# The rotated partner of mixer C's queries and keys, from four transfers within SBUF

## The chip, the cores and the metric

The kernel runs on one core of one Trainium2 chip. The metric is the device time of one execution in microseconds; the lower one is the better one. The kernel before takes 1890.34 us (median of three runs, 1889.98 to 1893.89).

## What is computed

The reference is a trunk of two layers over 512 tokens of 2,048 features, all in float32. Each layer norms its input with a modulation that is computed from a vector `c`, projects it once to 6,656 columns, runs four kinds of attention on disjoint columns, gates their outputs and projects them back. Cut to the parts that the change meets:

```python
for i in range(DEPTH):                                   # 2
    mod = silu(c) @ w_ada[i] + b_ada[i]
    h = rms_norm(x, norm_w[i]) * (1 + scale) + shift
    proj = h @ w_in[i]                                   # 2048 x 6656
    y_a, y_b, y_c, y_d = four mixers on their columns    # 8 heads of 64 each
    y = concat(y_m * silu(z_m) for the four mixers)
    x = x + gate * (y @ w_out[i])
return rms_norm(x, final_norm_w)

def apply_rope(x, cos, sin):         # mixer C: q (8 heads) and k (2 heads), after rms_norm
    x0, x1 = x[..., 0::2], x[..., 1::2]                  # adjacent pairs of a head
    return stack([x0 * cos - x1 * sin, x0 * sin + x1 * cos], -1)
```

The angles depend on the token's row (first 16 pairs of a head) or column (last 16 pairs) in a grid 64 wide. Scores are sums over a head's 64 features, so any order of the features that is the same in q and k gives the same scores.

## The kernel before

Activations lie with features on the 128 partitions and the 512 tokens along the row. The weights come as blocks of 128 x 128, eight to a load (`wst`, 512 KB). A block times an activation tile is a *step*; it takes three matmuls, since weights and activations are each split into a high and a low part (`wh`, `wl`, `hh`, `hl`): ACT copies the high part, DVE subtracts to get the low part (`w_conv`, line 185). There are 2,224 steps: 52 output tiles of the input projection and 16 of the output projection, 16 steps each, twice, and some halved ones. The trace names their PSUM tiles `pj0qD`, `pj1o` and so on: layer, kind, mixer.

The program is written by a planner that runs at build time. `slot` (line 147) emits four steps, 12 matmuls, and among them the pieces of other work, which are generators that say after how many slots, and at which of the places 0 to 4 in the slot, they go on. A *unit* (line 958) is the attention of one head for 128 queries: scores `s` on PE, then on DVE the bias and the row's extreme (for mixer C a maximum), the exponential on ACT, a reciprocal on DVE, the scaling on ACT; two slots after the scores come the transposes `pt` on PE, then a copy on ACT and a subtraction on DVE, and with every second unit the value products `o`. At most one unit starts in a slot, and only while `lag` is under `THR[0]`, 2000. `lag` is the planner's own account: `Meter` (line 89) adds an assumed price for each instruction that goes through it, and at a slot's end (line 168) `lag` grows by DVE's sum and falls by PE's, or by 1000 if that is more.

A finished projection is worked off by a generator of its kind: `ev_rope` for q and k of mixer C (line 869), `ev_q`, `ev_k`, `ev_v`, `ev_z`. One starts in a slot, and until it is through, its PSUM bank of eight is held. They need SBUF buffers from rings: `tmp` (4), `qs` (6), and `b4` (11 of 4 KB a partition), which holds keys, values, transposed probabilities and the tiles of `w_ada`. `ev_k` waits until 2 + `RES` = 6 of `b4` are free (line 790), `ev_v` for mixers B and D until 5 are (line 797); a unit with an even number takes two of them at its transposes. `ada_tick` (line 263) streams `w_ada` through `b4` and gives DVE its products. Before a projection tile is opened, `open_proj` (line 714) puts in empty slots, with no steps, until three PSUM banks are free.

After the first weight group a scheduler may still move instructions against each other; each engine then works its own list in order. All loads are issued by SP. Every compute instruction has line 101 in the trace, since `Meter` records it there (line 105 in the changed program).

In `ev_rope` the square goes to `sq` and the normed weight times the input to `qw`; `st` sums squares per head on PE, and `ro` is the product of `qw` with a 128 x 128 sign matrix `rot`, which puts minus x1 in the place of x0 and x0 in that of x1. DVE then forms `ro` times sine, `qw` times cosine and their sum; the rotation is done for 5 tiles in each layer, 10 in all.

Of the kernel before, what the change touches and what calls it, by code (L numbers as in the profile page):

```python
# [18 lines left out]
F32 = mybir.dt.float32  # L19
# [3 lines left out]
ALU = mybir.AluOpType  # L23
# [39 lines left out]
NP, TP, LP, VP = (0, 1), (1, 0), (0, 1), (1, 2)  # L63
THR = (2000, 1200)
MAGIC = float(0x5F3759DF)


def col0(name):
# [43 lines left out]
class Trunk:  # L112
# [249 lines left out]
    def setup(self):  # L362
        nc, io, p = self.nc, self.io, self.p
        names = (("c", 16), ("nw", 32), ("bada", 96), ("qw", 2), ("kw", 2), ("fw", 16), ("sink", 16))
        vt = p.tile([128, sum(n for _, n in names)], F32, name="vec")
        nc.sync.dma_start(vt, io["vec"])
        self.vec, o = {}, 0
        for n, k in names:
            self.vec[n] = vt[:, o:o + k]
            o += k  # L370
        ct = p.tile([128, 128 + 128 + 112 + 2 + 1], F32, name="cst")
        nc.sync.dma_start(ct, io["cst"])
        self.ident, self.rot, self.maskb, self.bones = ct[:, :128], ct[:, 128:256], ct[:, 256:368], ct[:, 368:370]
        self.ones = ct[:, 370:371]
        self.x = []
        for k in range(KT):
            t = p.tile([128, 512], F32, name=f"x{k}", tag="y", bufs=16)
            nc.sync.dma_start(t, io["xT"][k * 128:(k + 1) * 128, :])
            self.x.append(t)
        self.ada_seq = []  # L380
        for k in range(KT):
            self.ada_seq += [(0, 16 + k, 0), (0, 16 + k, 1), (0, k, 0), (0, k, 1)]
        self.ada_seq += [(0, 32 + k, hf) for k in range(KT) for hf in range(2)]
        self.ada_seq += [(1, k, hf) for k in range(48) for hf in range(2)]
        self.ada_issued = self.ada_done = 0
        self.ada_t = deque()
        self.ada_every = None
        self.ada_last = 0
        self.ada_keep = 0
        self.ada_dma(4)  # L390
        self.wst, self.wc, self.wdma, self.wcn = {}, {}, 0, 0
        for g in range(2):
            self.w_dma(g)
        self.half1 = p.tile([128, 48], F32, name="half1")
        self.mod = [p.tile([128, 48], F32, name=f"mod{l}") for l in range(NL)]
        self.am = [p.tile([128, 16], F32, name=f"am{l}") for l in range(NL)]
        self.nsink = p.tile([128, 16], F32, name="nsink")
        self.ccol = p.tile([128, 16], F32, name="ccol")
        self.cond = p.tile([128, D], F32, name="cond")
        self.cos = p.tile([128, 512], F32, name="cos")  # L400
        self.sin = p.tile([128, 512], F32, name="sin")
        nc.scalar.activation(self.ccol, self.vec["c"], AF.Tanh, scale=0.5)
        nc.vector.scalar_tensor_tensor(self.ccol, self.ccol, 1.0, self.vec["c"], op0=ALU.add, op1=ALU.mult)
        nc.vector.tensor_scalar(self.nsink, self.vec["sink"], -1.0, None, op0=ALU.mult)
        rows = [self.new_ps(f"cr{q}") for q in range(4)]
        for q in range(KT):
            nc.tensor.matmul(rows[q // 4][:, (q % 4) * 128:(q % 4 + 1) * 128], self.ccol[:, q:q + 1].to_broadcast([128, 128]),
                             self.ident, start=True, stop=True)
        for k in range(KT):
            self.add_square(self.x[k], k)  # L410
            if k % 4 == 3:
                q = k // 4
                nc.scalar.activation(self.cond[:, q * 512:(q + 1) * 512], rows[q], AF.Copy)
        self.end_ps(4)
        ps = self.new_ps("warm")
        self.keep_warm(ps, self.x[KT - WARM[0]:KT])
        self.end_ps()
        self.ada_do()
        self.ada_do()
        self.rstd = self.rms_rows((self.ada_do, self.ada_do, lambda: self.ada_am(0)))  # L420
        self.ada_dma(DEPTH0)
# [447 lines left out]
    def ev_rope(self, l, kind, j, ps, rel):  # L869
# [5 lines left out]
        nc.scalar.activation(sq, ps, AF.Square)  # L875
        nc.scalar.activation(qw, ps, AF.Copy, scale=w)
        rel()
        yield 1, 1
        while self.ps_free < 2:
            yield 1, 1  # L880
        st = self.new_ps(f"st{self.uid()}")
        for i in range(4):
            nc.tensor.matmul(st[:, 2 * i:2 * i + 2], sq[:, i * 128:(i + 1) * 128], self.bones, start=True, stop=True)
        r = self.p.tile([128, 16], F32, name=f"rq{self.uid()}", tag="rq", bufs=6)
        pr = self.new_ps(f"ro{self.uid()}")
        nc.tensor.matmul(pr, self.rot, qw, start=True, stop=True)
        self.r_tmp.put()
        yield 0, 3
        self.rsqrt(st[:, :8], 8, 1.0 / 64, 0.125 if kind == "q" else 1.0, r[:, :8], nc.gpsimd)
        nc.vector.tensor_tensor(tr, pr, self.sin, op=ALU.mult)  # L890
        self.end_ps(2)
        yield 1, 3
        nc.vector.tensor_tensor(qw, qw, self.cos, op=ALU.mult)
        nc.vector.tensor_tensor(tr, tr, qw, op=ALU.add)
        self.r_tmp.put()
# [233 lines left out]
def constants():  # L1129
    onehot, d = bucket_onehot()  # L1130
    n = np.abs(d)
    gmask = np.zeros((16, 1024), np.float32)
    gmask[:8] = np.where(n <= 128, 0.0, NEG)
    cnt = (n <= 64).astype(int) + ((n <= 256) & (n % 4 == 0)) + (n % 16 == 0)
    gmask[8:] = np.where(cnt > 0, np.log(np.maximum(cnt, 1)), NEG)
    dw = np.arange(16)[:, None]
    mb = np.full((16, 112), NEG, np.float32)
    for o, blk, w0, n_ in ((0, 0, 0, 32), (32, 1, 0, 48), (80, 3, 32, 32)):
        w = 16 * blk + dw
        key = (w0 if blk != 1 else 0) + np.arange(n_)[None, :]  # L1140
        st = np.clip(w - 8, 0, 48)
        mb[:, o:o + n_] = np.where((key >= st) & (key < st + 16), 0.0, NEG)
    rot = np.zeros((128, 128), np.float32)
    for i in range(0, 128, 2):
        rot[i + 1, i] = -1.0
        rot[i, i + 1] = 1.0
    bones = np.zeros((128, 2), np.float32)
    bones[:64, 0] = 1.0
    bones[64:, 1] = 1.0
    cst = np.concatenate([np.eye(128, dtype=np.float32), rot, np.tile(mb, (8, 1)), bones,  # L1150
                          np.ones((128, 1), np.float32)], 1)
    t = np.arange(L)
    inv = (np.float32(10000.0) ** (-np.arange(0, 32, 2, dtype=np.float32) / np.float32(32))).astype(np.float32)
    ang = np.concatenate([(t // 64).astype(np.float32)[:, None] * inv, (t % 64).astype(np.float32)[:, None] * inv], 1)
    idx = (np.arange(128) % 64) // 2
    return {"onehot": onehot, "gmask": gmask, "cst": np.ascontiguousarray(cst.astype(np.float32)),
            "cos": np.ascontiguousarray(np.cos(ang).astype(np.float32).T[idx]),
            "sin": np.ascontiguousarray(np.sin(ang).astype(np.float32).T[idx])}


def lay_out(inp, steps):
    g = {k: np.asarray(v) for k, v in inp.items()}
    w = np.empty((NSTEP, 128, 128), np.float32)
    for s, (mat, l, t, k) in enumerate(steps):
        c = col0(t) if mat == "in" else 128 * t
        w[s] = g["w_in" if mat == "in" else "w_out"][l, k * 128:(k + 1) * 128, c:c + 128]
    pad = np.zeros((NL, 8, 15, 63), np.float32)
    pad[..., 16:47] = g["na_rpb"]
    rpb = np.stack([pad[..., 15 - dw:63 - dw] for dw in range(16)], 2)
    cols = lambda a: a.reshape(a.shape[0], -1, 128).transpose(2, 0, 1).reshape(128, -1)  # L1170
    vec = np.concatenate([
        cols(g["c"]), cols(g["norm_w"]), cols(g["b_ada"]), np.tile(g["q_norm_w"], (1, 2)).T, np.tile(g["k_norm_w"], (1, 2)).T,
        cols(g["final_norm_w"][None]), np.broadcast_to(g["attn_sink"].reshape(1, 16), (128, 16))], 1)
    wada = np.ascontiguousarray(g["w_ada"].reshape(NL, 2, 1024, 48, 128).transpose(0, 3, 1, 4, 2))
    arrays = {
        "w": np.ascontiguousarray(w.reshape(NGRP, GW, 128, 128).transpose(0, 2, 1, 3)).reshape(NGRP, 128, GW * 128),
        "wada": wada,
        "xT": np.ascontiguousarray(g["x"][0].T),
        "c": np.ascontiguousarray(g["c"]),
        "vec": np.ascontiguousarray(vec),  # L1180
        "rpb": np.ascontiguousarray(rpb.reshape(NL, 128, 15, 48)),
        "t5": np.ascontiguousarray(g["t5_table"]),
    }
    arrays.update(constants())
    return arrays


SHAPES = {"w": (NGRP, 128, GW * 128), "wada": (NL, 48, 2, 128, 1024), "xT": (D, L), "c": (1, D), "vec": (128, 180),
          "rpb": (NL, 128, 15, 48), "t5": (32, 16), "onehot": (32, 1024), "gmask": (16, 1024), "cst": (128, 371),
          "cos": (128, 512), "sin": (128, 512)}  # L1190


# [17 lines left out]
```

## Time and profile before

| | us |
|---|---|
| median of three runs | 1890.34 |
| profiled execution | 1894.71 |
| its span, first to last instruction | 1892.9 |
| PE busy in the span | 1854.4 (98%) |
| DVE busy | 1356.3 (72%) |
| ACT busy | 1078.2 (57%) |
| chain that ended last: PE's share | 88% |
| 20 matmuls of `ro`, median of one | 0.634 |

The profile is one execution. A matmul is pipelined and its end is modelled, so what one costs in the stream is read from the starts around it, not from its duration. A product in plain float32 stands in the trace as two instructions, one in the program. The program's list orders instructions and tells no times; the trace tells the times.

### The profile page before, as it was taken

What the parts mean: (1) busy time and instruction counts of PE and PEld (TensorE: products, weight loads), DVE (VectorE), ACT (ScalarE), POOL (GpSimd) and SP (SyncE); (2) the same over time, 40 slices, a digit from 0 to 9 for tenths busy, and PEclk for the clock granted to TensorE, in tenths of its full rate; (3) what the DMA queues carried; (4) which work ended last, traced back from release to release, by engine and by line L of the source; (5) the groups of instructions that cost most, each with busy time, mean ns of one, the idle gap of its engine ahead of it and who ended that gap; (6) DMA issues with size and microseconds to landing.
All of it is one profiled execution on the core that took longest, in us unless ns stands there. A gap on an engine that the chain in (4) does not pass through costs nothing.

```text
span 1892.9 us, 26325 instructions
## 1 busy us (share of the span) xinstructions
PE 1854.4 (98%) x9256; PEld 1546.5 (82%) x9256; DVE 1356.3 (72%) x2861; ACT 1078.2 (57%) x2186; POOL 59.5 (3%) x144
## 2 busy tenths in 40 slices
PE   7999999999999999999999999999999999999997
PEld 5787788888888888888778888888888888888887
DVE  7998988787676768977776775577757666655336
ACT  5342457777777776622245773477656666655333
POOL 0001110100000000000000000210000000000000
PEclk8999999999999999999999999999999999999999
DMA  9897544251133226688833333322334342232335
GB/s 335 320 347 233 203 164 135 91 189 60 65 97 109 94 87 223 241 280 305 285 105 129 122 124 139 111 79 90 112 120 127 111 128 89 88 99 89 134 120 181
DMA packets 91459, 291.44 MB, mean 154 GB/s; under 512 B 10208, under 2 KB 17888, under 8 KB 91328
## 3 DMA queue, kind: packets, MB, share of 16 engines
q1 hardware_dynamic: 91328, 289.76, 45.2%
q8 instruction: 73, 1.20, 0.3%
q14 instruction: 58, 0.48, 0.1%
HBM read 278.57 MB, written 11.16 MB: 153 GB/s over the span
## 4 chain that ended last, share of the span: by engine, by line
PE 88%; DVE 7%; DMA 2%; ACT 2%; issue 2%; SPq 0%; DVEq 0%; ACTq 0%
PE pj1o L101 9%; PE pj0o L101 8%; PE o L101 5%; PE s L101 5%; PE pt L101 4%; DVE b L101 3%; PE pj0qB L101 2%; PE pj1zA L101 2%; PE pj1zC L101 2%; PE pj0kB L101 2%; PE pj1zB L101 2%; PE pj1qB L101 2%; PE pj1vD L101 2%; PE pj1qC L101 2%; PE pj1zD L101 2%; PE pj1qA L101 2%
## 5 line engine op out<-in xcount | busy, mean ns | idle before, releaser
L101 ACT ACTIVATE wh<-wst 128x512 fp32r<-128x512 f32 x556 | 346.5, 626 | 398.4 <-PE pj1o L101 77.3
L101 DVE TENSOR_TENSOR wl<-wst,wh 128x512 fp32r<-128x512 f32 x556 | 383.7, 691 | 261.9 <-ACT wh L101 227.1
L101 ACT ACTIVATE P<-P,sm 128x512 f32<-128x512 f32 (+2 forms) x384 | 245.7, 641 | 135.2 <-DVE sm L101 133.5
L101 PE MATMUL s<-b,qs 128*128 128x512 f32 (+2 forms) x512 | 158.9, 392 | 0.2 <-DVE sm L101 0.2
L101 DVE TENSOR_TENSOR b<-pt,b 128x512 fp32r<-128x512 f32 (+2 forms) x256 | 149.4, 584 | 0.8 <-ACT b L101 0.3
L101 DVE CUSTOM_DVE_ANT_0 b<-b,cond,vec 128x1024 f32<-128x1024 f32 x96 | 123.3, 1285 | 28.5 <-DMA b<-wada 28.2
L101 PEld LDWEIGHTS o<-b,b 128*128 128x128 f32 x896 | 124.5, 190 | 13.3 <-DVE b L101 2.9
L101 PEld LDWEIGHTS pt<-cst,P 128*128 128x128 f32 x832 | 106.7, 140 | 34.6 <-ACT P L101 1.3
L101 PE MATMUL pt<-cst,P 128*128 128x128 f32 x832 | 132.4, 272 | 0.9 <-ACT P L101 0.9
L101 ACT ACTIVATE b<-pt 128x512 fp32r<-128x512 f32 (+2 forms) x256 | 129.8, 507 | 2.3
L101 DVE CUSTOM_DVE_ANT_0 b<-b,cond,half 128x1024 f32<-128x1024 f32 x96 | 122.9, 1280 | 4.6 <-DMA b<-wada 3.7
L101 PE MATMUL o<-b,b 128*128 128x256 f32 (+1 forms) x896 | 123.7, 278 | 2.3 <-DVE b L101 2.3
L101 PE MATMUL pj1o<-yh,wh 128*128 128x512 f32 (+1 forms) x304 | 108.6, 357 | 0.0
L101 PE MATMUL pj1o<-yl,wh 128*128 128x512 f32 (+1 forms) x304 | 108.2, 356 | 0.0
L101 PE MATMUL pj1o<-yh,wl 128*128 128x512 f32 (+1 forms) x304 | 108.2, 356 | 0.0
L101 PE MATMUL pj0o<-yh,wl 128*128 128x512 f32 x256 | 100.4, 392 | 1.1 <-DVE wl L101 1.1
L101 PE MATMUL pj0o<-yh,wh 128*128 128x512 f32 x256 | 100.0, 391 | 0.0
L101 PE MATMUL pj0o<-yl,wh 128*128 128x512 f32 x256 | 99.8, 390 | 0.0
L101 DVE TENSOR_TENSOR ot<-o,ot 64x256 f32<-64x256 f32 x109 | 46.0, 422 | 56.0 <-ACT ot L101 54.7
L101 DVE RECIPROCAL sm<-sm 128x1 f32<-128x1 f32 x256 | 41.5, 162 | 62.0 <-ACT P L101 59.2
L101 PEld LDWEIGHTS s<-b,qs 128*128 128x128 f32 x512 | 78.9, 190 | 2.2 <-DVE sm L101 0.4
L101 ACT ACTIVATE P<-s,sm,rq 128x512 f32<-128x512 f32 x64 | 49.8, 778 | 44.2 <-DVE sm L101 43.9
(365 smaller groups left out, 4409.7 us busy)
## 6 DMA issues: line engine op xcount, KB each, us to landing
wst<-w SPq DMA_DIRECT2D x278, 512.0 KB, 3.5
b<-wada SPq DMA_DIRECT2D x192, 512.0 KB, 6.1
T<-btab SPq DMA_DIRECT2D x16, 448.0 KB, 5.3
T<-gtab SPq DMA_DIRECT2D x16, 448.0 KB, 5.0
x<-xT SPq DMA_DIRECT2D x16, 256.0 KB, 5.4
tmp<-xT SPq DMA_DIRECT2D x16, 256.0 KB, 5.5
xs<-xn SPq DMA_DIRECT2D x16, 256.0 KB, 2.5
out<-xn SPq DMA_DIRECT2D x32, 128.0 KB, 1.8
```

The costliest lines, as they stand in the source:

```text
L101: return f(*a, **k)
```

## The change

The sign matrix leaves the constant table, which shrinks from 371 to 243 columns. The columns of C's q and k in the weights are sorted on the host (`PAIRS`): in each head the first members of the 32 pairs come first and then the second members, so a value's partner lies 32 partitions away. In `ev_rope`, as soon as `qw` is written, four transfers of 32 partitions by 512 columns on SP's queue copy each block of `qw` to the place of its partner in `tr`. The sign has moved into the sine table. The product `ro` and its PSUM bank are gone; `tr` times sine is now formed in place by DVE, in the slot of the other two operations, one slot later than before.

```diff
--- before.py
+++ after.py
@@ -65,6 +65,10 @@
 MAGIC = float(0x5F3759DF)
 
 
+
+PAIRS = np.arange(128).reshape(2, 32, 2).transpose(0, 2, 1).reshape(-1)
+
+
 def col0(name):
     kind, m, j = name[0], name[1], int(name[2])
     return BASE[m] + OFFS[m][kind] + 128 * j
@@ -368,10 +372,10 @@
         for n, k in names:
             self.vec[n] = vt[:, o:o + k]
             o += k
-        ct = p.tile([128, 128 + 128 + 112 + 2 + 1], F32, name="cst")
+        ct = p.tile([128, 128 + 112 + 2 + 1], F32, name="cst")
         nc.sync.dma_start(ct, io["cst"])
-        self.ident, self.rot, self.maskb, self.bones = ct[:, :128], ct[:, 128:256], ct[:, 256:368], ct[:, 368:370]
-        self.ones = ct[:, 370:371]
+        self.ident, self.maskb, self.bones = ct[:, :128], ct[:, 128:240], ct[:, 240:242]
+        self.ones = ct[:, 242:243]
         self.x = []
         for k in range(KT):
             t = p.tile([128, 512], F32, name=f"x{k}", tag="y", bufs=16)
@@ -875,21 +879,21 @@
         nc.scalar.activation(sq, ps, AF.Square)
         nc.scalar.activation(qw, ps, AF.Copy, scale=w)
         rel()
+        for o in range(0, 128, 32):
+            nc.sync.dma_start(tr[o:o + 32], qw[o ^ 32:(o ^ 32) + 32])
         yield 1, 1
-        while self.ps_free < 2:
+        while self.ps_free < 1:
             yield 1, 1
         st = self.new_ps(f"st{self.uid()}")
         for i in range(4):
             nc.tensor.matmul(st[:, 2 * i:2 * i + 2], sq[:, i * 128:(i + 1) * 128], self.bones, start=True, stop=True)
         r = self.p.tile([128, 16], F32, name=f"rq{self.uid()}", tag="rq", bufs=6)
-        pr = self.new_ps(f"ro{self.uid()}")
-        nc.tensor.matmul(pr, self.rot, qw, start=True, stop=True)
         self.r_tmp.put()
         yield 0, 3
         self.rsqrt(st[:, :8], 8, 1.0 / 64, 0.125 if kind == "q" else 1.0, r[:, :8], nc.gpsimd)
-        nc.vector.tensor_tensor(tr, pr, self.sin, op=ALU.mult)
-        self.end_ps(2)
+        self.end_ps()
         yield 1, 3
+        nc.vector.tensor_tensor(tr, tr, self.sin, op=ALU.mult)
         nc.vector.tensor_tensor(qw, qw, self.cos, op=ALU.mult)
         nc.vector.tensor_tensor(tr, tr, qw, op=ALU.add)
         self.r_tmp.put()
@@ -1140,36 +1144,33 @@
         key = (w0 if blk != 1 else 0) + np.arange(n_)[None, :]
         st = np.clip(w - 8, 0, 48)
         mb[:, o:o + n_] = np.where((key >= st) & (key < st + 16), 0.0, NEG)
-    rot = np.zeros((128, 128), np.float32)
-    for i in range(0, 128, 2):
-        rot[i + 1, i] = -1.0
-        rot[i, i + 1] = 1.0
     bones = np.zeros((128, 2), np.float32)
     bones[:64, 0] = 1.0
     bones[64:, 1] = 1.0
-    cst = np.concatenate([np.eye(128, dtype=np.float32), rot, np.tile(mb, (8, 1)), bones,
+    cst = np.concatenate([np.eye(128, dtype=np.float32), np.tile(mb, (8, 1)), bones,
                           np.ones((128, 1), np.float32)], 1)
     t = np.arange(L)
     inv = (np.float32(10000.0) ** (-np.arange(0, 32, 2, dtype=np.float32) / np.float32(32))).astype(np.float32)
     ang = np.concatenate([(t // 64).astype(np.float32)[:, None] * inv, (t % 64).astype(np.float32)[:, None] * inv], 1)
-    idx = (np.arange(128) % 64) // 2
+    idx = np.arange(128) % 32
+    sign = np.where(np.arange(128) % 64 < 32, np.float32(-1), np.float32(1))[:, None]
     return {"onehot": onehot, "gmask": gmask, "cst": np.ascontiguousarray(cst.astype(np.float32)),
             "cos": np.ascontiguousarray(np.cos(ang).astype(np.float32).T[idx]),
-            "sin": np.ascontiguousarray(np.sin(ang).astype(np.float32).T[idx])}
+            "sin": np.ascontiguousarray(np.sin(ang).astype(np.float32).T[idx] * sign)}
 
 
 def lay_out(inp, steps):
     g = {k: np.asarray(v) for k, v in inp.items()}
     w = np.empty((NSTEP, 128, 128), np.float32)
     for s, (mat, l, t, k) in enumerate(steps):
-        c = col0(t) if mat == "in" else 128 * t
-        w[s] = g["w_in" if mat == "in" else "w_out"][l, k * 128:(k + 1) * 128, c:c + 128]
+        c = (col0(t) if mat == "in" else 128 * t) + (PAIRS if mat == "in" and t[:2] in ("qC", "kC") else np.arange(128))
+        w[s] = g["w_in" if mat == "in" else "w_out"][l][k * 128:(k + 1) * 128, c]
     pad = np.zeros((NL, 8, 15, 63), np.float32)
     pad[..., 16:47] = g["na_rpb"]
     rpb = np.stack([pad[..., 15 - dw:63 - dw] for dw in range(16)], 2)
     cols = lambda a: a.reshape(a.shape[0], -1, 128).transpose(2, 0, 1).reshape(128, -1)
     vec = np.concatenate([
-        cols(g["c"]), cols(g["norm_w"]), cols(g["b_ada"]), np.tile(g["q_norm_w"], (1, 2)).T, np.tile(g["k_norm_w"], (1, 2)).T,
+        cols(g["c"]), cols(g["norm_w"]), cols(g["b_ada"]), np.tile(g["q_norm_w"], (1, 2)).T[PAIRS], np.tile(g["k_norm_w"], (1, 2)).T[PAIRS],
         cols(g["final_norm_w"][None]), np.broadcast_to(g["attn_sink"].reshape(1, 16), (128, 16))], 1)
     wada = np.ascontiguousarray(g["w_ada"].reshape(NL, 2, 1024, 48, 128).transpose(0, 3, 1, 4, 2))
     arrays = {
@@ -1186,7 +1187,7 @@
 
 
 SHAPES = {"w": (NGRP, 128, GW * 128), "wada": (NL, 48, 2, 128, 1024), "xT": (D, L), "c": (1, D), "vec": (128, 180),
-          "rpb": (NL, 128, 15, 48), "t5": (32, 16), "onehot": (32, 1024), "gmask": (16, 1024), "cst": (128, 371),
+          "rpb": (NL, 128, 15, 48), "t5": (32, 16), "onehot": (32, 1024), "gmask": (16, 1024), "cst": (128, 243),
           "cos": (128, 512), "sin": (128, 512)}
 
 
```

The first rotation of layer 0 in PE's list, before. `st` is the sum of squares, `pj0qC` the projection that runs meanwhile.

```order
L101 MATMUL pj0qC0_2090<-hh0_8_845,wl74_2065 128x512
L101 MATMUL st29_2148<-cst_68,tmp50_2124 128x2 x4
L101 MATMUL ro31_2154<-tmp51_2125,cst_68 128x512
L101 MATMUL pj0qC0_2090<-hh0_9_926,wh74_2064 128x512
L101 MATMUL pj0qC0_2090<-hl0_9_927,wh74_2064 128x512
```

And now:

```order
L105 MATMUL pj0qC0_2090<-hh0_8_845,wl74_2065 128x512
L105 MATMUL st29_2152<-cst_68,tmp50_2124 128x2 x4
L105 MATMUL pj0qC0_2090<-hh0_9_926,wh74_2064 128x512
L105 MATMUL pj0qC0_2090<-hl0_9_927,wh74_2064 128x512
L105 MATMUL pj0qC0_2090<-hh0_9_926,wl74_2065 128x512
```

`ro` is gone and the rest stands as it stood.

PE's list after the last matmul of `pj0qD3` in layer 0, which is the 2,304th projection matmul of either program. Before:

```order
L101 MATMUL pj0qD3_7221<-hh0_15_1676,wl191_7230 128x512
L101 MATMUL pt522_7393<-cst_68,P117_7316 128x128 x4
L101 MATMUL s523_7405<-b4235_6985,qs36_7076 128x512 x2
L101 MATMUL pj0vD3_7388<-hh0_0_256,wh192_7265 128x512
L101 MATMUL pj0vD3_7388<-hl0_0_257,wh192_7265 128x512
L101 MATMUL pj0vD3_7388<-hh0_0_256,wl192_7266 128x512
```

Now, with the first rows, four from the middle and the last ones (105 matmuls lie between the two projections):

```order
L105 MATMUL pj0qD3_6681<-hh0_15_1676,wl191_6690 128x512
L105 MATMUL pt427_6832<-cst_68,P94_6767 128x128 x2
L105 MATMUL s428_6836<-b4215_6550,qs30_5613 128x384 x2
...
L105 MATMUL pt445_6949<-cst_68,P98_6932 128x128 x4
L105 MATMUL s446_6955<-b4225_6919,qs31_6040 128x512 x2
L105 MATMUL pt448_6965<-cst_68,P99_6940 128x128 x4
L105 MATMUL s449_6971<-b4225_6919,qs31_6040 128x512 x2
...
L105 MATMUL s468_7091<-b4226_6920,qs32_6041 128x512 x2
L105 MATMUL pt470_7109<-cst_68,P105_7093 128x128 x4
L105 MATMUL o471_7116<-b4233_7069,b4192_5749 128x256
L105 MATMUL pj0vD3_6902<-hh0_0_256,wh192_6723 128x512
```

Before, one set of transposes and one pair of scores lie between the projections of `pj0qD3` and `pj0vD3`; now ten units' scores and their transposes and value products do.

DVE's list at the first q rotation of layer 1, before (`wl` are conversions of weights, `rs` belongs to the norm):

```order
L101 TENSOR_TENSOR wl352_11876<-wst177_11773,wh352_11875 128x512
L101 TENSOR_SCALAR rs736_11896<-st733_11882 128x8
L101 TENSOR_SCALAR rs736_11896<-rs736_11896 128x8 x2
L101 TENSOR_TENSOR tmp181_11863<-ro735_11888,sin_123 128x512
L101 TENSOR_TENSOR tmp180_11862<-tmp180_11862,cos_122 128x512
L101 TENSOR_TENSOR tmp181_11863<-tmp181_11863,tmp180_11862 128x512
L101 TENSOR_TENSOR wl353_11921<-wst177_11773,wh353_11920 128x512
```

And now:

```order
L105 TENSOR_SCALAR rs729_11910<-st727_11898 128x8
L105 TENSOR_SCALAR rs729_11910<-rs729_11910 128x8 x2
L105 TENSOR_TENSOR wl353_11934<-wst177_11785,wh353_11933 128x512
L105 TENSOR_TENSOR tmp181_11875<-tmp181_11875,sin_123 128x512
L105 TENSOR_TENSOR tmp180_11874<-tmp180_11874,cos_122 128x512
L105 TENSOR_TENSOR wl354_11955<-wst178_11832,wh354_11954 128x512
L105 TENSOR_TENSOR tmp181_11875<-tmp181_11875,tmp180_11874 128x512
```

The product with the sine has moved behind one conversion, `wl353`, and one conversion, `wl354`, now stands between the cosine and the sum.

## Rows read from the trace of the kernel before

**Rows 1.** Page, busy times: us, share of the span, instructions.

```profile
PE 1854.4 (98%) x9256; PEld 1546.5 (82%) x9256; DVE 1356.3 (72%) x2861; ACT 1078.2 (57%) x2186; POOL 59.5 (3%) x144
```

**Rows 2.** Timeline of PE at a rotation: start us, us, then the instruction.

```profile
1171.09 0.39 PE L101 MATMUL pj1zB<-hh,wl 128*128 128x512 f32 x1
1171.32 0.95 PE L101 MATMUL st<-cst,tmp 128*128 128x2 f32 x8
1172.12 1.10 PE L101 MATMUL ro<-tmp,cst 128*128 128x512 f32 x2
1172.67 0.80 PE L101 MATMUL pj1zB<-hh,wh 128*128 128x512 f32 x1
1173.30 0.40 PE L101 MATMUL pj1zB<-hl,wh 128*128 128x512 f32 x1
```

**Rows 3.** Tile `ro`: count, ns min/median/max, first and last start us.

```profile
L101 PE MATMUL ro<-tmp,cst x20: 592/634/676, 246.1 to 1272.8; 128*128 128x512 f32 x20
```

**Rows 4.** Timeline of PE, one attention unit among projections in layer 0.

```profile
702.24 0.60 PE L101 MATMUL pt<-cst,P 128*128 128x128 f32 x4
702.59 0.72 PE L101 MATMUL s<-b,qs 128*128 128x512 f32 x2
703.14 0.40 PE L101 MATMUL pj0qD<-hh,wh 128*128 128x512 f32 x1
...
704.52 1.11 PE L101 MATMUL o<-b,b 128*128 128x256 f32 x8
705.47 0.39 PE L101 MATMUL pj0qD<-hh,wh 128*128 128x512 f32 x1
```

**Rows 5.** DVE by form, 400 to 720 us: busy us, mean ns | idle.

```profile
L101 DVE TENSOR_TENSOR b<-pt,b 128x512 fp32r<-128x512 f32 x48 | 32.8, 682 | 0.1
...
L101 DVE CUSTOM_DVE_ANT_0 P<-s,T 128x512 f32<-128x512 f32 x22 | 15.1, 687 | 0.4
...
L101 DVE RECIPROCAL sm<-sm 128x1 f32<-128x1 f32 x79 | 12.8, 162 | 23.7 <-ACT P L101 23.5
...
L101 DVE TENSOR_TENSOR b<-pj0kD,b 64x512 fp32r<-64x512 f32 x16 | 11.0, 687 | 0.4
...
L101 DVE DVE_READ_ACCUMULATOR2_ANT sm<- 128x1 f32 x54 | 4.4, 82 | 0.0
```

**Rows 6.** ACT groups by form, 400 to 720 us.

```profile
L101 ACT ACTIVATE P<-P,sm 128x512 f32<-128x512 f32 x70 | 50.4, 719 | 21.2 <-DVE sm L101 21.0
...
L101 ACT ACTIVATE b<-pt 128x512 fp32r<-128x512 f32 x48 | 28.1, 584 | 0.4
...
L101 ACT ACTIVATE b<-pj0kD 64x512 fp32r<-64x512 f32 x16 | 9.4, 590 | 0.2
...
L101 ACT ACTIVATION_READ_ACCUMULATOR P<-P,sm 128x1 f32 x21 | 3.9, 187 | 0.0
```

**Rows 7.** Timeline of PE at the end of layer 0's projections.

```profile
765.84 0.60 PE L101 MATMUL vt<-cst,tmp 128*128 128x128 f32 x4
766.20 0.48 PE L101 MATMUL pj0o<-yh,wh 128*128 128x512 f32 x1
```

**Rows 8.** Windows: stretch, busy PE, PEld, DVE, ACT, POOL, then PEclk, DMA, GB/s.

```profile
19.00:20.00 1.00, 1.00 (x3) 0.40 (x2) 0.87 (x3) 0.00 (x0) 0.00 (x0) 0.50 1.02 410
```

**Rows 9.** Timeline of PE in the load stage.

```profile
14.65 5.49 PE L101 MATMUL warm<-x,cst 128*128 128x512 f32 x6 [4.08 <-DMA x<-xT]
```

**Rows 10.** Timeline of all engines at a rotation in layer 1.

```profile
1205.07 0.68 ACT L101 ACTIVATE tmp<-pj1qC,vec 128x512 f32<-128x512 f32 x1
...
1205.43 0.33 SPq L181 DMA_DIRECT2D wst<-w  x1
...
1209.43 0.69 DVE L101 TENSOR_TENSOR tmp<-ro,sin 128x512 f32<-128x512 f32 x1 [0.39 <-PE ro L101]
```

**Rows 11.** Page, DMA issues: KB each, median us from issue to landing.

```profile
wst<-w SPq DMA_DIRECT2D x278, 512.0 KB, 3.5
...
out<-xn SPq DMA_DIRECT2D x32, 128.0 KB, 1.8
```

## The prediction

> **What bounds the kernel now.** I read the page's busy times first: TensorE (PE) is busy for 98% of the span [rows 1]. A busy PE need not be a dense one, so I then read PE's stream in order of time. In it the projection matmuls start 0.23 us apart, and the small products of the attention units stand between them without a gap [rows 2, 4]. So the end is set by PE's stream: a product that leaves it shortens the run by its own place in it, and a stretch in which PE has nothing in its queue that may start lengthens the run by the whole gap. VectorE (DVE) and ScalarE (ACT) are hidden as long as projections lie between the units.
>
> **What goes.** The rotation product `ro` is ten instructions of the program and 20 in the trace [rows 3]. Around one: `st` starts at 1171.32, `ro` at 1172.12, the next projection matmul but one at 1173.30. Without `ro` that one would start 0.23 after its predecessor, so `ro` holds the stream for 1173.30 - 1172.12 - 0.23 = 0.95 us [rows 2]. Ten times: **-9.5 us**. All of it is on the path.
>
> **What comes.** Forty transfers of 64 KB on SP's queue and a wait of DVE for them. In layer 1 the operand is ready at 1205.75 (1205.07 + 0.68) and DVE comes to the product with the sine at 1209.43, after waiting 0.39 for `ro`; an issue holds SP's queue for 0.33 [rows 10]. Four of them end at 1207.1, and a landing of 1.8, as for the 128 KB stores [rows 11], is 1208.9: in time. At 3.5, as for the 512 KB weight loads, DVE would stand for about 1.2 us per rotation with weight conversions queued behind it; these run three slots ahead of PE, and that covers it. I count 0, with 0 to +10 us in all as bounds. The place of a transfer behind a weight load that waits for DVE decides nothing either: the load waits for a conversion that stands ahead of the rotation in DVE's order. The page "DMA: Bandwidth & Descriptors" of the Trainium skill (section "Anatomy of one DMA — SWDGE (gpsimd) path") gives a fixed cost of about 2.0 us per transfer plus its bytes; by it these would land after an estimated 2.2 us. The trace's smaller transfers agree with that size (1.8), and by either the wait is hidden. The shorter constant table, the sorted weight columns and the signed sine table change no instruction: 0. DVE does the same three operations per rotation, two of them a slot later than the first; 0 by itself.
>
> **What moves, and why it is dear.** The planner books DVE and PE time in `lag`. With the product gone from PE's account and all three DVE operations in one slot, its own counters, followed through both programs, part at slot 80: `lag` is 1234 before and 2614 now, over the limit of 2000. The first unit of head A1 is held back, and every later unit of layer 0 is one slot late, while the projections and the loads for the modulation are not. At slot 122 that swaps two claims. A unit with an even number takes two `b4` buffers at its transposes; before, such a unit stood there, and of the 5 free buffers 3 were left. Now an odd one stands there, 5 are free, and mixer B's second value tile, which asks for 5, takes one. Mixer B's first key tile, which asks for 6, is passed over then and again after: its keys come at slot 149 and not at 128. Units stand still meanwhile, finished projections keep their PSUM banks, and `open_proj`, which wants three free banks, inserts empty slots: 40 more than before, all in layer 0. Projections run ahead of their cover and the units come later without it. The order of the built programs shows it: PE has 105 matmuls, none of a projection, after the 2,304th projection matmul, where before six stood (excerpt in the section on the change), and two shorter such stretches after the 2,016th and the 2,160th. Layer 1 has the same plan as before.
>
> **Price of the long stretch.** Ten units start in it (two of B, eight of D), two older ones end, and three key tiles are split, two of them at its end. PE's work: transposes 0.35 per four, scores 0.55 per pair, value products 0.95 per eight [rows 4]: for eight D units 2.8 + 4.4 + 2.85, for the B units and their leftovers some 3.5 by their smaller sizes; 13.5 us. The time: one D unit is scores 0.55, minimum on DVE 0.69 + 0.08, exponential on ACT 0.72 + 0.19, reciprocal 0.16, scaling 0.72, transposes 0.35 [rows 4 to 6]: 3.5 us until the unit after next may send its scores, since these stand behind the transposes in PE's order. Two units are in flight, and copies (0.58) and subtractions (0.68) of the others queue in front. Walking the rows of PE, DVE and ACT in their order, each started when its engine and its releaser are done, I get 13.7 us to the first D unit's minimum (four B units drain, then four subtractions of 0.69 for the keys), and 26.4 us for the eight D units with the second key split, 40.1 in all. PE is late by 40.1 - 13.5 = **+26.6 us**. Bounds: with DVE packed (some 30 us of its rows before the last scores) +16.5; with the units wholly one after another (ten of 5.2, copies and value products included, and two key splits of 4 x 0.59 + 4 x 0.69 = 5.1) +49. I take the walk, which follows the order that will run.
>
> **The other stretches**, walked in the same way with B's smaller tiles: after 2,160, four B units, 8.7 us for 4.6 of work, **+4.1**; after 2,016, 4.5 for 2.6, **+1.9**; at the end of the projections (2,496) one unit is left over, **+1.5**. An empty slot without a unit costs nearly nothing: three stand before 766.20 in the old program, where PE goes from `vt` to `pj0o` in 0.36 [rows 7]. For the three single ones I take **+0.5**.
>
> **The clock.** In the load stage the granted clock stands at 0.50 (1.2 GHz) from 19 to 20 us, though PE has been at work again since 14.65, after 4.08 us without any [rows 8, 9]; dense work at that level takes twice its time. PE will stop for 2 to 5 us several times in the long stretch. What a fall costs is mostly paid after it, when projections return at half speed: I count one fall, with half of 5 us (14.65 to 20) lost, **+2.5**; bounds 0 and +10 (the 0.35 + 0.55 on each D unit's chain doubled, eight times, and the 2.5). The page "TensorE: Matmul & The Clock Gate" of the Trainium skill ("A second HAM failure mode: psum-queue depth-cycling") says that short idle times between groups of matmuls make the clock swing between its levels; by it the long stretch would be at the lower level throughout, which is the third rival.
>
> **Sum:** -9.5 + 26.6 + 4.1 + 1.9 + 1.5 + 0.5 + 2.5 = **+27.6 us**. The profiled execution took 1894.7 (span 1892.9), 4.4 over the median of 1890.3 of the runs; the sum gives 1922.3 against it and 1917.9 against the median. I forecast **1918**.
>
> **Rivals.**
> - *The stretches cost nothing* (0.04): the units' work on DVE and ACT was done early, and PE only makes up order. For it: PE was 98% busy, the amount of PE work is the same. Against: no unit can start before its scores. Then 1890.3 - 9.5 = 1881, faster. It decides if stretches without projections take under 9 us more than their PE work.
> - *The two cancel* (0.03): walks too long by three times; 1887 to 1894.
> - *The clock stays down* (0.08): 1.2 GHz through all three stretches and for 5 us after each: 0.9 more per unit on the chain, 17 units of which half are smaller, some 12, and two recoveries more, 5; 1918 + 17 = 1935. Against: in the span's middle the trace has no such stretch to show it.
> - *Transfers land late* (0.06): the transfers wait in SP's queue or land at 3.5 and more, and in the slots with units DVE's stand reaches PE: 10 x 1.2 to 2 us, 1930 to 1938. Against: the landing of the small stores above.
>
> The forecast itself has 0.79, with 1903 to 1935 as its own range. The range for eight in ten takes in most of the clock and transfer cases: **1903 to 1940**. Faster by over 0.2% (3.8 us, about what a measurement can tell from no change) 0.04, within it 0.03, slower 0.93.
>
> **What would show it.** Right: PE busy share falls in one stretch of some 40 us in the middle of layer 0 (about 600 to 800 us) with `s`, `pt` and `o` alone, ended by waits for ACT and DVE; layer 1 is shorter by five times 0.95; `tmp<-tmp` lands within 3 us. Wrong: PE dense there (first rival), DVE's idle time before the sine product ended by a DMA for over 2 us (fourth), a clock of 0.50 for over 10 us (third). The forecast fails if the units in the long stretch follow each other in under 2 us or over 4.5.

## The result: slower by 2.6%, 21 us more than forecast

The changed kernel takes 1940.49 us (median of four runs, 1939.21 to 1946.06), the kernel before 1892.12 on the same chip: a ratio of 1.0262, 95% interval 1.0249 to 1.0274, so +48.4 us where +27.6 had been forecast. The direction and its cause held; the time lies 0.5 us above the range that ended at 1940, and 22.5 above the 1918 forecast, which had been counted from 1890.34. The profiled execution is the longest of the four, 1946.06 against 1939.21 to 1941.14 for the others; its span is 1944.3 where it was 1892.9, +51.4. The account below is made between these two spans and so holds some 3 us more than the medians differ by.

The page's busy times after, for [rows 1]:

```profile
PE 1870.9 (96%) x9236; PEld 1556.7 (80%) x9236; DVE 1357.6 (70%) x2861; ACT 1082.5 (56%) x2186; POOL 57.8 (3%) x144
```

PE has lost its ten products and yet is busy for 16.5 us longer, and its share has fallen from 98 to 96%: time in which it worked slowly and time in which it stood. Where, the windows show (stretch, busy PE, PEld, DVE, ACT, POOL, then the granted clock, DMA share, GB/s):

```profile
600.00:620.00 20.00, 16.86 (x84) 13.28 (x84) 13.78 (x33) 14.15 (x33) 0.00 (x0) 0.91 0.44 145
...
700.00:720.00 20.00, 11.94 (x49) 8.63 (x48) 12.70 (x33) 12.52 (x28) 0.00 (x0) 0.66 0.18 50
720.00:740.00 20.00, 12.94 (x61) 9.85 (x59) 12.09 (x31) 15.18 (x32) 0.00 (x0) 0.74 0.17 53
```

The loss lies in layer 0's middle, as forecast: PE is busy for under 25 of the 40 us from 700 to 740, and the granted clock there is 0.66 and 0.74 in the mean, more than the one fall that had been counted. The long stretch after the 2,304th projection matmul, PE in order of time:

```profile
701.30 0.40 PE L105 MATMUL pj0qD<-hh,wl 128*128 128x512 f32 x1
...
701.67 0.59 PE L105 MATMUL s<-b,qs 128*128 128x384 f32 x2
703.49 0.89 PE L105 MATMUL o<-b,b 128*128 128x256 f32 x6 [1.22 <-DVE sm L105]
...
705.84 0.51 PE L105 MATMUL s<-b,qs 128*128 128x256 f32 x2 [1.11 <-DVE ot L105]
...
718.90 1.11 PE L105 MATMUL pt<-cst,P 128*128 128x128 f32 x4 [3.95 <-ACT P L105]
...
743.85 0.63 PE L105 MATMUL pj0vD<-hh,wh 128*128 128x512 f32 x1
```

From the last projection (701.30) to the next (743.85) are 42.55 us; the walk had said 40.1. PE waits for `P` from ACT (3.95 at 718.90, then 2.62 and 3.91), the chain of the units, as forecast. But at 703.49 and 705.84 it waits for something else: value products and scores stand for DVE's `sm` and `ot`, which are no inputs of theirs. The reading is that each of these takes over the PSUM bank that DVE reads there for the last time; the trace names no banks, and the run with four banks below tests it. The first short stretch shows little but that:

```profile
604.10 0.39 PE L105 MATMUL pj0vD<-hh,wl 128*128 128x512 f32 x1
604.33 0.38 PE L105 MATMUL pt<-cst,P 128*128 128x128 f32 x2
604.47 0.60 PE L105 MATMUL s<-b,qs 128*128 128x384 f32 x2
606.18 0.44 PE L105 MATMUL pt<-cst,P 128*128 128x128 f32 x2 [1.12 <-DVE sm L105]
606.61 0.59 PE L105 MATMUL s<-b,qs 128*128 128x384 f32 x2
607.95 0.89 PE L105 MATMUL o<-b,b 128*128 128x256 f32 x6 [0.75 <-DVE sm L105]
608.67 0.52 PE L105 MATMUL pt<-cst,P 128*128 128x128 f32 x3
610.30 0.51 PE L105 MATMUL s<-b,qs 128*128 128x256 f32 x2 [1.12 <-DVE ot L105]
...
611.79 0.80 PE L105 MATMUL pj0qD<-hh,wh 128*128 128x512 f32 x1
```

The units here have two banks at most, since empty slots are put in while fewer than three are free: `pt` at 606.18 takes the bank of the `s` at 604.47 and stands 1.12 until DVE has formed its minimum; `o` at 607.95 takes the next `s`'s; `s` at 610.30 takes `o`'s. Together 3.0 of the 7.69 us. In all of layer 0's attention such waits come to 8.8 us (3.2 + 3.1 + 1.7 + 0.8 in the waits of 300 to 960 us; columns: total us, times, longest):

```profile
PE pt L105 <- ACT P L105: 17.5, 10, 3.9
PE s L105 <- DVE ot L105: 3.2, 3, 1.1
PE o L105 <- DVE sm L105: 3.1, 3, 1.2
PE pt L105 <- DVE sm L105: 1.7, 2, 1.1
...
PE s L105 <- DVE sm L105: 0.8, 2, 0.5
```

The rotation itself did what was said of it. In layer 1, for [rows 2]:

```profile
1228.66 0.95 PE L105 MATMUL st<-cst,tmp 128*128 128x2 f32 x8
...
1229.80 0.40 PE L105 MATMUL pj1zB<-hl,wh 128*128 128x512 f32 x1
```

From `st` to the second projection matmul behind it 1.14 us, 1.98 before: a product was worth 0.84, not 0.95, since without it the second matmul behind `st` starts 0.33 after the first and not 0.23. Over layer 1's five rotations the same projection matmuls take 4.24 us less, 0.85 each. For [rows 10 and 11], the queue and the landing of the transfers:

```profile
1261.57 0.68 ACT L105 ACTIVATE tmp<-pj1qC,vec 128x512 f32<-128x512 f32 x1
...
1262.35 2.41 SPq L883 DMA_DIRECT2D tmp<-tmp  x4
```

```profile
tmp<-tmp SPq DMA_DIRECT2D x40, 64.0 KB, 2.8
```

Four issues hold SP for 2.41 (0.60 each, not 0.33), they land after 2.8 at the median, not 1.8, and the product with the sine waited for one of them 0.2 us in all, in ten rotations. The page "DMA: Bandwidth & Descriptors" of the Trainium skill ("Anatomy of one DMA — SWDGE (gpsimd) path") would put it at an estimated 2.2, by a fit for transfers that GpSimd issues; these are SP's, and the trace has 0.6 more. Neither reaches the path.

Two places had no term. One is the first `kb` product of layer 0, which now comes up 1.65 us before its root from GpSimd is ready:

```profile
255.52 1.09 PE L105 MATMUL kb<-cst,rq 128*64 128x128 f32 x16 [1.65 <-POOL rq L298]
```

The other is the boundary of the layers. PE there before, from the sums `cs` to the first projection, and then after:

```profile
954.57 0.95 PE L101 MATMUL cs<-cst,b 128*128 128x1 f32 x8
...
957.15 2.82 PE L101 MATMUL rb<-tmp,cst 128*128 128x512 f32 x6
...
962.47 0.50 PE L101 MATMUL pj1kA<-hh,wh 128*128 128x512 f32 x1 [1.59 <-ACT hh L101]
```

```profile
1006.91 1.87 PE L105 MATMUL cs<-cst,b 128*128 128x1 f32 x8 [2.09 <-DVE b L105]
...
1011.93 5.40 PE L105 MATMUL rb<-tmp,cst 128*128 128x512 f32 x6
...
1019.82 0.50 PE L105 MATMUL pj1kA<-hh,wh 128*128 128x512 f32 x1 [1.59 <-ACT hh L105]
```

The stand of 2.09 for DVE is new, and behind it everything to 1017.17 runs at a granted clock of 0.50, the three broadcasts `rb` in 5.40 and not 2.82. DVE is late since it waited 1.44 us for the last but one reload of the residual, which SP had issued at 998.93:

```profile
1004.72 0.75 DVE L105 SCALAR_TENSOR_TENSOR xn<-pj0o,mod,tmp 128x512 f32<-128x512 f32 x1 [1.44 <-DMA tmp<-xT]
```

SP had been issuing `w_ada` up to 991.04, 16 us before `cs`; in the kernel before it issued the last at 924.84, 30 us ahead of it.

### The profile page after: what moved, and what is told of

It is laid out like the page before. It is cut to its first block, busy times and chain, and to the rows that moved or that the text cites. A ratio compares the mean times of both kernels' runs of the same rounds, so it can differ in the third digit from the quotient of the medians.

```text
span 1944.3 us, 26358 instructions
## 1 busy us (share of the span) xinstructions
PE 1870.9 (96%) x9236; PEld 1556.7 (80%) x9236; DVE 1357.6 (70%) x2861; ACT 1082.5 (56%) x2186; POOL 57.8 (3%) x144
## 4 chain that ended last, share of the span: by engine, by line
PE 80%; DVE 8%; DMA 6%; issue 3%; ACT 2%; SPq 0%; POOL 0%; DVEq 0%; ACTq 0%
PE pj1o L105 9%; PE o L105 5%; PE s L105 5%; PE pt L105 5%; DVE b L105 4%; DMA b<-wada 3%; PE pj0o L105 3%; DMA tmp<-xT 2%; PE pj1zA L105 2%; PE pj0kB L105 2%; PE pj1zB L105 2%; PE pj1zC L105 2%; PE pj0vD L105 2%; PE pj0vB L105 2%; PE pj1qD L105 2%
## 5 line engine op out<-in xcount | busy, mean ns | idle before, releaser
L105 PE MATMUL pt<-cst,P 128*128 128x128 f32 x832 | 137.5, 279 | 19.5 <-ACT P L105 17.5
L105 PEld LDWEIGHTS o<-b,b 128*128 128x128 f32 x896 | 128.6, 197 | 19.5 <-ACT b L105 3.3
L105 PE MATMUL o<-b,b 128*128 128x256 f32 (+1 forms) x896 | 129.8, 285 | 6.4 <-DVE sm L105 3.1
```

The lines of the kernel that those rows point to most:

```text
L105: return f(*a, **k)
```

## The experiments

Each ran beside the kernel before on the same chip; ratios are to it, with 95% intervals. All are edits of the changed kernel, except the second.

**The account put back.** The planner's books alone: PE is charged a product that no longer exists, and DVE's sine product is charged where it used to stand.

```diff
+        nc.tensor.ns += 0.42 * 512                # at st
+        nc.vector.ns += 100 + 1.04 * 512          # in the old slot
         yield 1, 3
         nc.vector.tensor_tensor(tr, tr, self.sin, op=ALU.mult)
+        nc.vector.ns -= 100 + 1.04 * 512
```

> The four transfers stay, the product stays gone, but the planner's account is put back: PE is booked the product's 215 ns and DVE's product with the sine is booked in its old slot, so that the units stand in the slots of the kernel before and the empty slots are 12 again, not 52. Theory (the whole loss is the plan): the time before less ten products of 0.82 to 0.95 us, 1892.1 - 8.2 to 9.5 = 1882.6 to 1884, and no fall of the clock in the middle of layer 0. Rival (the transfers and the later sine product carry part of the loss): above 1892.

1885.06 us, ratio 0.9963 (0.9950 to 0.9977): 55 us under the changed kernel, 7.7 under the kernel before. The transfers are all there, and so is the product's gain, less the 1.65 of the `kb` product, which stands here too; the upper end of the expectation was passed by 1 us. PE's longest waits in layer 0's attention, and a window of its middle, with the clock at 1.00:

```profile
PE pt L105 <- ACT P L105: 1.4, 2, 0.9
```

```profile
700.00:720.00 20.00, 19.83 (x107) 16.58 (x106) 15.47 (x33) 15.95 (x33) 0.00 (x0) 1.00 0.26 80
```

**The product kept, the new account.** The mirror image, made from the kernel before.

```diff
         nc.tensor.matmul(pr, self.rot, qw, start=True, stop=True)
+        nc.tensor.ns -= 0.42 * 512
...
         nc.vector.tensor_tensor(tr, pr, self.sin, op=ALU.mult)
+        nc.vector.ns -= 100 + 1.04 * 512
...
         nc.vector.tensor_tensor(qw, qw, self.cos, op=ALU.mult)
+        nc.vector.ns += 100 + 1.04 * 512
```

> The kernel before with its rotation product, without any transfer, but with the account of the changed kernel (215 ns less for PE, the sine product booked a slot later): the same 52 empty slots at the same places. Theory (the plan alone loses the time): the changed kernel's 1940.5 plus ten products, 1948 to 1950. Rival (the transfers cost it): 1892, as before.

1946.40, ratio 1.0280 (1.0264 to 1.0296), 1.6 us below the 1948 to 1950 expected. Not one instruction was added or taken from the kernel before, and it lost 54 us. Its long stretch (704.2 to 746.8) has the same 42.55 us and the same waits, among them:

```profile
721.79 1.11 PE L101 MATMUL pt<-cst,P 128*128 128x128 f32 x4 [3.95 <-ACT P L101]
```

With the first experiment this is a square of two by two: the plan costs 54 to 55 us with either way of rotating, the transfers gain 6 to 8 with either plan.

**The limit at 2700 and at 2600.**

```diff
-THR = (2000, 1200)
+THR = (2700, 1200)      # and 2600
```

> The changed kernel with one number changed: a unit may start while lag is under 2700 instead of 2000, so that the 2614 at slot 80 no longer holds head A1 back; 12 empty slots. Theory: 1882 to 1885, within 2 us of the run with the account put back. Rival (without the product the planner's stretches come anyway): about 1940.

> The same with a limit of 2600, just under the 2614 of slot 80: 49 empty slots. Theory (one unit held back at slot 80 sets off the rest): 1915 to 1945, far from the run with 2700. Rival (it is the general level of the limit that counts): close to the run with 2700, 1883.

2700 gives 1884.82, ratio 0.9960 (0.9947 to 0.9972); 2600 gives 1941.18, ratio 1.0253 (1.0239 to 1.0267). A hundred units of the planner's own account, on either side of the 2614 at slot 80, are worth 56 us. At 2700 PE waits for `P` in layer 0's attention for 1.3 us in all. So the loss starts at a decision that falls between the two limits, and the unit held back at slot 80 is one; no run excludes that another lies there too. This version and the one with the account put back beat the kernel before by 0.4% and the changed one by 55 us; they differ from each other by less than their intervals.

**The key before the value.**

```diff
-... self.r_b4.free < 1 + (RES_C if m in "AC" else RES):
+... self.r_b4.free < 1 + (RES_C if m in "AC" else RES + (m == "B" and ("B", 0) not in self.kk)):
```

> The changed kernel with one condition added: a value tile of mixer B asks for one more free buffer as long as B's first key tile is not in place, so it can't take the buffer that the key waits for. The unit at slot 80 is still held back. 18 empty slots instead of 52. Theory (the swap of those two claims is the link that makes the loss): 1883 to 1895. Rival (a late unit costs it, by whatever buffer): 1915 or more.

1902.84, ratio 1.0056 (1.0034 to 1.0077), above the 1895 expected. The swap of the two claims carries 38 of the 55 us, not all: 18 empty slots remain where 12 were, and two stretches with them, 12.42 us after the 1,440th projection matmul (427.7 to 440.1) and 6.77 after the 2,304th (714.6 to 721.4). PE's waits between 300 and 960:

```profile
PE pt L105 <- ACT P L105: 11.2, 7, 3.2
```

**PE's gaps filled.** To price the clock, one more product ahead of each set of transposes in an empty slot; it is thrown away.

```diff
+        if l == 0 and self.in_idle:
+            self.nc.tensor.eng.matmul(pt, self.ident, self.cos, start=True, stop=True)
```

> The changed kernel, with one more product (identity times the cosine table, 128x512, plain float32, thrown away: the transposes overwrite its bank) in front of a unit's transposes wherever these stand in an empty slot of layer 0: 22 of them, some 0.9 us of PE each at full clock. They need nothing that PE waits for and so lie in its idle time. Theory (half of the unforecast loss is the clock that falls in the stretches: 22 us of work done at half rate): the clock is at 1.2 GHz for under 20 us in all between 600 and 1020 us, where it was for over 54, and the time falls to 1925 to 1936. Rival (the chain over DVE and ACT sets the stretches and PE's clock in them costs nothing): no gain, or 1940 to 1960 for the added products.

23 such products ran. 1936.71, ratio 1.0237 (1.0214 to 1.0261), 0.7 us above the range expected and not clear of the changed kernel's interval; the clock did what was expected (at 0.50 for 13.7 us between 600 and 1020, where it was for 54.6):

```profile
700.00:720.00 20.00, 15.56 (x71) 9.31 (x70) 14.94 (x36) 14.57 (x33) 0.00 (x0) 1.00 0.18 48
720.00:740.00 20.00, 16.13 (x69) 11.50 (x69) 15.88 (x33) 14.66 (x30) 0.00 (x0) 0.83 0.17 50
```

The long stretch took 37.61 us with twelve added products in it, against 42.55 without. So the lower clock costs some 5 us there at least, and most of the stretch is there without it: the windows still show PE at work for only 31.7 of 40 us, added products included. How much more than 5, this kernel can't say, since the products themselves cost something.

**Residual reloads on ACT's queue.**

```diff
-        nc.sync.dma_start(r[:, cs], src[rows, cs])
+        (nc.scalar.eng if l == 0 and j > 12 else nc.sync).dma_start(r[:, cs], src[rows, cs])
```

> The changed kernel, with the last three reloads of the residual tile in layer 0's output projection issued by ACT instead of SP, so that they no longer stand behind weight loads, modulation loads and stores in SP's queue. Theory (the 8 us lost at the boundary of the layers come from the last reload's late issue, which makes PE idle for 5.7 us there and so lowers its clock): the wait of the sums for DVE at the boundary (2.1 us) is gone, the clock stays at 1.00 there, and the time is 1931 to 1935. Rival (the boundary is late because DVE itself is behind): the wait and the fall stay, 1940.

1938.65, ratio 1.0239 (1.0224 to 1.0255): in the profile the place is mended, in the median no gain is clear of the intervals.

```profile
1000.19 0.95 PE L105 MATMUL cs<-cst,b 128*128 128x1 f32 x8
...
1008.09 0.50 PE L105 MATMUL pj1kA<-hh,wh 128*128 128x512 f32 x1 [1.59 <-ACT hh L105]
```

From `cs` to the first projection 7.90 us, as before the change, not 12.91, no stand for DVE, and the clock at 1.00. Late reloads are thus the cause of the stand. The time expected, 1931 to 1935, was missed: the profiled execution took 1936.56, the others 1938.35 to 1939.35. This trace also differs from the changed kernel's elsewhere, without any edit there: it is 2.0 us later in the load stage, 2.4 longer in layer 1, and its clock did not fall behind the stretches after the 1,104th and the 2,016th projection matmul.

The fall of the clock at the boundary is another matter. In the profiles of three runs of this section it falls at the same `rb` though PE did not stand for DVE there, as in *Three times the transfers*:

```profile
950.02 0.95 PE L105 MATMUL cs<-cst,b 128*128 128x1 f32 x8
...
953.02 5.47 PE L105 MATMUL rb<-tmp,cst 128*128 128x512 f32 x6
```

In *The key before the value* `rb` took 4.52, in *Four banks* 4.27. So one profile without the fall does not show that the reloads made it. Of the boundary's 7.1 us the stand and a longer wait behind it (1.42 for 0.72) are 2.8, and the other 4.3 go with the clock, whose cause there stays open. In the median the edit gained 1.8 us, within the intervals; what the boundary is worth there is not shown.

**Three times the transfers**, on the kernel with the account put back.

```diff
+            for _ in range(3):
                 nc.sync.dma_start(tr[o:o + 32], qw[o ^ 32:(o ^ 32) + 32])
```

> The kernel with the account put back, but each of the 40 transfers within SBUF is issued three times, so that a rotation's twelve hold SP's queue for some 7 us instead of 2.4 and land some 5 us later. Theory (the transfers are hidden with several us of slack): DVE waits at the product with the sine, for under 2 us per rotation, PE hardly; 1883 to 1890. Rival (they are at the edge, and only the empty slots hide that in the changed kernel): 1900 to 1930.

1885.34, ratio 0.9964 (0.9952 to 0.9976), no different from one time. Twelve issues hold SP for 7.5 to 9.3 us, and the sine product waited 0.2 us in all, once:

```profile
  DMA tmp<-tmp: 0.2, 1
```

The last of a rotation's transfers is thus issued some 6 us later than with four, and that is hidden still.

**Four banks.**

```diff
-        while self.ps_free < (1 if self.s < 8 else 3):
+        while self.ps_free < (1 if self.s < 8 else 4):
```

> The changed kernel, but an output tile is opened only with four PSUM banks free, not three: the empty slots are 53 and not 52 and lie earlier, and in the stretches after the 1,824th, 1,968th and 2,112th projection matmul three banks go round among the units, where two did after the 2,016th and 2,160th. Theory (what the walk of the short stretches missed are waits for a bank: PE's scores, transposes and value products stand until DVE has left the only other one): PE's waits for DVE at these three kinds of product, 8.8 us in the changed kernel, fall below 4, and the short stretches lose less each; the time 1930 to 1940, since the long one stays. Rival (the waits are the units' own chain over DVE and ACT, and a third bank changes nothing): 8 us or more of such waits, 1940 or more.

1939.35, ratio 1.0251 (1.0233 to 1.0268). The stretch after the 1,824th projection matmul holds the very instructions of the changed kernel's after the 2,016th, with three banks in place of two:

```profile
559.75 0.40 PE L105 MATMUL pj0kD<-hh,wl 128*128 128x512 f32 x1
...
560.56 0.38 PE L105 MATMUL pt<-cst,P 128*128 128x128 f32 x2
561.84 0.61 PE L105 MATMUL s<-b,qs 128*128 128x384 f32 x2 [0.90 <-DVE sm L105]
562.29 0.81 PE L105 MATMUL o<-b,b 128*128 128x256 f32 x6
564.35 0.55 PE L105 MATMUL pt<-cst,P 128*128 128x128 f32 x3 [1.25 <-ACT P L105]
...
565.67 0.50 PE L105 MATMUL pj0vD<-hh,wh 128*128 128x512 f32 x1
```

5.92 us from projection to projection where it was 7.69 (the last 0.8 of that at a clock of 0.50). Over layer 0's attention the waits for a bank fall from 8.8 to 2.4 us (1.8 below and 0.6 of `pt`), as expected of them, and those for ACT's `P` rise from 17.5 to 24.9:

```profile
PE pt L105 <- ACT P L105: 24.9, 18, 3.2
...
PE s L105 <- DVE sm L105: 1.8, 2, 0.9
```

The kernel as a whole is no faster, but that says little of the banks: its empty slots lie elsewhere, with stretches of 8.6 and 8.7 us after the 1,104th and the 1,440th projection matmul, where the changed kernel has 3.35 and none, and a long one of 35.9.

## Why the forecast was wrong in size, and what of it held

**What held** is the mechanism of the plan: a limit at slot 80, the swap of two claims of `b4` (38 of the 55 us), empty slots, PE without projections, and nothing lost to the transfers. The square of the first two experiments and the pair of limits show it. The prediction's signs for it came too: a stretch of some 40 us with waits for ACT and DVE, and transfers that land within 3 us. What failed is the price of three things in the sum.

**The sizes**, profiled execution against profiled execution:

| term | forecast | measured |
|---|---|---|
| ten products gone | -9.5 | -8.4 |
| long stretch, after 2,304 | +26.6 | +28.8 |
| after 2,160 | +4.1 | +8.0 |
| after 2,016 | +1.9 | +4.9 |
| after 2,496 | +1.5 | +2.7 |
| single empty slots (after 1,104) | +0.5 | +1.7 |
| the clock, behind the stretches | +2.5 | +6.5 |
| boundary of the layers | none | +7.1 |
| `kb` waits for GpSimd | none | +1.7 |
| the rest, by difference, mostly in the load stage and layer 1 | | -1.6 |
| sum | +27.6 | +51.4 |

A stretch's measured cost is the time from the last projection matmul to the next, less 0.23 and less the work of PE that the prediction priced: 42.55 - 0.23 - 13.5, 12.85 - 0.23 - 4.6, 7.69 - 0.23 - 2.6. For the last two it names no work, and an estimate from the rows stands in its place: 5.87 - 0.23 - 2.9, and after the 1,104th 3.35 - 0.23 - 0.55 less the 0.9 that stood there before. The boundary is 12.91 for 7.90 us and the stand of 2.09.

**The step that failed first** is the pricing of the stretches beside the long one, "walked in the same way": 8.0 forecast, 17.3 measured (8.0 + 4.9 + 2.7 + 1.7). The walk started each row when its engine and its releaser were done, but it knew only data as a releaser, no banks. Waits for a bank are 6.2 of the missing 9.3 us: 3.0 after 2,016 and 3.2 after 2,160. In the two smallest stretches PE stood for data, 2.35 for ACT's `P` after 1,104 and 1.74 for DVE's `b` after 2,496. The last experiment bears the reading of the banks out; how much of these waits more banks would give back in the kernel's time, no run shows. The page "Perfetto Trace Analysis" of the Trainium skill ("Optimizing Tensor Performance") asks that independent matmul groups rotate through different PSUM banks; 5.92 against 7.69 us for the same rows is what came with the third bank here.

The long stretch came out near its 26.6 by luck in part. It has 2.3 us of bank waits that the walk did not know, and over half of it ran at half the clock that the walk assumed; with its gaps filled it took 37.6 us, added products included, under the 40.1 of the walk. So the walk was too long by 2.5 us or more for rows at full clock, and what it left out filled that up.

**The clock** was the second such term: one fall, half of 5 us, +2.5. Behind four stretches projections ran at half speed, as after the 2,160th and the long one, and inside the long one the clock stood at 0.50 without a break for 23.9 us:

```profile
662.35:665.60 3.25, 3.25 (x10) 2.57 (x9) 2.14 (x5) 2.80 (x6) 0.00 (x0) 0.51 0.17 45
706.50:730.40 23.90, 15.70 (x53) 11.70 (x53) 14.18 (x35) 14.94 (x33) 0.00 (x0) 0.50 0.16 42
743.85:747.50 3.65, 3.65 (x13) 3.07 (x13) 2.54 (x4) 0.78 (x2) 0.00 (x0) 0.50 0.02 4
```

With 3.46 us at 317.34 and 2.61 at 611.79 the half-speed projections are 13 us, half of them lost, +6.5. To that come some 5 us or more within the long stretch, by the run with its gaps filled. This is the third rival, and its own sign, a clock of 0.50 for over 10 us, came: it was given 0.08 and held in good part, beside the forecast and not in its place. The page "TensorE: Matmul & The Clock Gate" of the Trainium skill ("A second HAM failure mode: psum-queue depth-cycling") speaks of a clock that swings between its levels, which the prediction took for the lower level throughout. The trace agrees with the swing: 0.50 from 706.5 to 730.4, 1.00 from there to 740.7, then 0.50 again, 27 of the stretch's 42.55 us in all.

**The boundary**, +7.1, had no term. The prediction says of the loads for the modulation only that they are not a slot late with the units, and does not follow them to the end of layer 0; there they run on to 16 us before `cs`, where it had been 30, and the reloads behind them on SP's queue come late. That explains the stand; the cause of the clock's fall there stays open.

**The other rivals.** No stretch was free of cost, nothing cancelled, and the transfers landed in time even three at a time: these are settled by the runs. The range ended half a microsecond too low; it had room for the clock or for late transfers, and none for waits for a bank or for SP's queue at the boundary.

## What to carry to other kernels

When a planner orders the program by an account of its own, an edit changes the account as well as the work: follow its counters to the first decision that comes out otherwise, and test the two apart by giving the new code the old entry. When a stretch without cover is priced by walking rows, walk the buffers as well: with two PSUM banks left, scores, transposes and value products wait for the reader of the product before. And follow work that is pushed back to the end of its queue, to see who stands behind it there.

## What was not expected of the hardware

A transfer of 64 KB between 32 partitions and 32 others held SP's queue for 0.58 us at the median (0.51 to 2.34 in the changed kernel; the weight load of 512 KB in [rows 10] held it for 0.33) and landed after 2.8 us at the median (1.9 to 5.5). 120 of them cost no more time than 40 (1885.34 and 1885.06).

At the boundary of the layers the same three broadcasts `rb` took 2.82 us in some profiles and 4.27 to 5.47 in others at a granted clock that had fallen to 0.50, with and without a stand of PE before them.
